# The sample group's window state in a one-step decoder kernel: copied from DRAM to DRAM during the first MLP instead of stored from attention's buffers

## The chip, the cores and the metric

The kernel runs on one core of a Trainium2 chip, as one launch. The metric is device time in microseconds (us), the median of several executions. In what follows PE is the tensor engine, DVE the vector engine, ACT the scalar engine, POOL the GpSimd engine and SP the sync engine. SP does no arithmetic: it issues DMA transfers in the order in which they stand in its program, and where one of them has to wait for a semaphore, all that stand behind it wait too. ACT and POOL can issue transfers as well.

## What is computed

One step of a two-layer trunk runs for two groups with the same weights. The prompt group is one sequence of 512 new tokens; the sample group is eight sequences (DEC_BATCH = 8) with one new token each and 2048 cached ones. The first layer mixes by pooling, then comes an MLP; keys and values are computed once; the second layer is attention over three branches (compressed rows, selected pages, a sliding window of 512) with 16 heads, then comes an MLP and the last norm.

```
h -> pool mixer -> sq_relu_mlp            (first layer)
k, v rows <- kv_side(h)
h -> attention(compressed, selected pages, window) -> sq_relu_mlp -> rmsnorm
outputs: y of both groups, the prompt group's new rows and buffers,
         the sample group's new rows, its pool buffer
         and its updated window buffer, win_kv_sample (8, 512, 2, 4, 64)
```

The last of these is what the change is about. In the kernel its key part and its value part are the DRAM tensors `o["wink"]` and `o["winv"]`, and the old window is `a_in["wink"]` and `a_in["winv"]`: each has 8 sequences of 512 KB, 4 MB in all. What is kept of the old window goes on unchanged to the updated buffer, 16 pieces of 512 KB in all.

## The kernel before

All numbers are float32. A product of weights with activations is made from two parts of each (`whi` and `wlo`, written by ACT and DVE), so one product of 1024 by 128 weights is 24 pairs of matmuls on PE.

**Phase A** (0 to about 597 us) holds the pooling layer, the first MLP and the compressed rows of the sample group's cache. `mlp_jobs` makes the MLP's list of jobs: four quarters of eight up products and eight down products. `Job.after` is code that is emitted right behind a job's work on PE. Weights come by SP into a ring of three buffers `wraw` of 512 KB (line 204), are split by ACT (line 215, `whi`) and by DVE (line 195, `wlo`), and the compressed rows' pages (`craw`, line 421) come on SP between them.

**Phase B** (to about 727 us) makes keys, values and queries. **Phase C** (727 to 961 us) is attention. **Phase D** is the output projection, the second MLP and the last norm.

In phase C one list scheduler orders everything (`attend` lists the steps, `emit` orders them). Each step has an engine, an estimated cost and a due time; on each engine that step is emitted which is due first among those that can start by the estimates. The two groups' work is mixed on PE in this way. For the prompt group PE computes scores (`sc`, line 1069), transposes of the weights (`pt`, line 1215) and products with the values (`pv`, line 1252), 28 `pv` matmuls per head. For the sample group PE reads 40 halves, which we number here:

- K0 to K3 are the scores against the window's keys, K4 to K19 those against the selected pages (line 1446, 16 `sv` matmuls each);
- V0 and V1 are the products with one half of the window's values, V2 to V17 those with the selected pages, V18 and V19 those with the other half of the window (line 1541).

Each half needs two buffers of 512 KB. They come from a ring of six, three `wraw` (the weights' buffers) and three `kvs`, filled by SP: a window's buffer by one transfer (line 1412), a pages' buffer by three or four transfers of one page (line 1417, a page's number read from a table first) while POOL fetches the page that is left (line 1421). So two buffers of pages are seven loads on SP.

For the window's halves there is a step more, `kept`: behind the PE step it puts on SP the two stores (`keep`, line 1433) of the same buffers into `o["wink"]` or `o["winv"]`, and then a step that stands for their transfer. Both touch the buffers, so to the scheduler a buffer is free only when the store is over. At the end of the phase SP loads the output projection's first weights into the three `wraw` buffers (line 204), and DVE's split of them (`wlo`) stands in DVE's order ahead of the sample group's last steps (`sx`, `sos`).

Of the kernel before, what the change touches and what calls it, by code (L numbers as in the profile page):

```python
# [17 lines left out]
NT = T + DB  # L18
# [7 lines left out]
# The list scheduler's aims in the attention phase, in microseconds: the end of head n is due at PERIOD * (n + 1) + LATE,  # L26
# the sample group's products evenly from FIRST on; BIAS shifts a head's kinds of steps against each other (scores,
# maxima, weights, sums, transposes, their high and low parts). ORDER: the chunks of the sample group's values.
# [4 lines left out]
# The order of the pooling layer: K a job of the sample group, s a step on the vector engine behind it, n the norm, u a  # L33
# product. FILLERS: the sample group's jobs behind each product of the first MLP.
# [3 lines left out]
# The order of the key and value products and the queries' with what stands between them; how many jobs later than the  # L38
# next each of their finishing steps comes; those whose rotation is the vector engine's.
# [8 lines left out]
class Buf:  # L48
    """One turn of a buffer: its kind, and the ops that touch it, the one that takes it among them."""
# [5 lines left out]
class Op:  # L55
    """A step on one engine: what emits it, about how long it takes, which ops it follows, which buffers it touches;
    due: when it has to be over, as far as its followers don't tell; lag: what its followers wait behind its end."""
# [9 lines left out]
def emit(ops, rings, taken=()):  # L67
    """Emits the ops as a list scheduler orders them: on each engine the one that is due first of those that can
    start. rings: buffers per kind; taken: buffers in use from the start."""
# [14 lines left out]
    def start(o):  # L84
        """The earliest start as far as it is known."""
        t = now
        for p in o.after:
            if p.end is None:
                return None
            t = max(t, p.end + p.lag)  # L90
        want = {}
        for b in o.bufs:
            old = turns[b.kind]
            if b in old:
                continue
            x = len(old) + want.get(b.kind, 0) - rings[b.kind]
            want[b.kind] = want.get(b.kind, 0) + 1
            if x >= 0:
                for u in old[x].users:
                    if u.end is None:  # L100
                        return None
                    t = max(t, u.end + 0.1)
        return t
# [29 lines left out]
class Job:  # L133
    """One stretch of work on the tensor engine, with what comes before it and after it. loads: (kind, function)
    pairs, one buffer each; frees: {kind: n}, the buffers that prep or pe is the last to read; post may be several
    functions, each a job later than the one before it; after comes right behind pe; no prep comes ahead of a job
    with bar."""
# [8 lines left out]
def trunk(tc, a, o):  # L146
# [17 lines left out]
    # ---- what lives through the whole program  # L164
# [32 lines left out]
    # ---- weights: raw from DRAM, then the two parts that float32r carries exactly  # L197
# [27 lines left out]
    def gemm(ps, w, xs, koff=0, m=128, cols=(0, 1)):  # L225
        """ps [m, 2, 512] = w' x over the k tiles; xs gives (hi, lo) [128, NT] of each."""
        n = len(xs)
        for k, (xh, xl) in enumerate(xs):
            for wt, x in ((w.hi, xh), (w.hi, xl), (w.lo, xh)):
                for i in cols:  # L230
                    TE.matmul(ps[0:m, i, 0:NH], wt[:, koff + k, 0:m], x[:, i * NH:(i + 1) * NH],  # L231
                              start=(k == 0 and wt is w.hi and x is xh), stop=(k == n - 1 and wt is w.lo))
# [5 lines left out]
    def run(js, ahead=1, done=0):  # L238
        """done: so many preps are out already."""
# [15 lines left out]
        def preps(i):  # L255
            """What is due once job i is on the tensor engine: the next ahead preps, none from behind a bar."""
# [44 lines left out]
    # ---- RMS norms  # L301
# [5 lines left out]
    def sq_acc(ct, rows=None):  # L307
        """Adds the squares of h's tile ct to the sums."""
        if ct == 0:
            S.activation(accn, h[:, 0], AF.Square)  # L310
            return
        q = tmp()
        S.activation(q, h[:, ct], AF.Square)
        V.tensor_add(accn, accn, q)
# [22 lines left out]
    def scaled(gi, ct):  # L337
        """The two parts of h's tile ct times the norm's weights; the products' columns take the rest of the norm."""
# [6 lines left out]
    # ================= phase A: pooling layer, first MLP, the sample group's compressed rows  # L345
# [49 lines left out]
    def pages(k, n):  # L395
        """The n page numbers from position k of the table."""
# [15 lines left out]
    def cmp_job(b, e, rq):  # L412
        """Two of the eight row pairs of one sequence's segments; the last one finishes the hidden rows."""
# [41 lines left out]
        # the values' rows: x0, x1 the even and the odd segments, A, B the two parts of the weights; a window of two  # L455
        # segments is A x0 + B x1 = (A - B) (x0 - x1) + A x1 + B x0 or A x1 + B x0 of the next pair
# [100 lines left out]
    def take(n):  # L557
        """The next n pieces of the sample group's work (a finishing step goes with the piece before it)."""
# [10 lines left out]
    # ---- pooling layer  # L569
# [6 lines left out]
    def first_norm():  # L576
        """h's sums of squares, added up on the tensor engine."""
# [110 lines left out]
    # ---- an MLP: four quarters of the hidden features, each summed into the residual  # L688
    def mlp_jobs(l, filler, done, before=lambda: None):
# [28 lines left out]
        for q in range(4):  # L718
            for f in range(8):
                js.append(gemm_job(W(a["up"][l, 8 * q + f]), xpairs, up_post(8 * q + f), kind=kind))  # L720
                if q == f == 0:
# [15 lines left out]
    def last_quarter(xs):  # L737
        """The last products and the final norm, one half of the rows after the other, so that the first half's norm and
        stores run beside the second half's products; the weights stay on chip for both."""
# [61 lines left out]
    # ================= phase B: K/V side and the queries  # L801
# [175 lines left out]
    # ---- queries: one head's two parts stacked on the partitions  # L977
# [82 lines left out]
    # ================= phase C: attention  # L1060
    hd_of = lambda t, s: ((2 * s + t // 4) * 4 + t % 4)

    def s_jobs(t, s):
        """Scores and weights of one head, for the query tiles 0 and 1, 2, 3: window and selected keys side by side, the
        compressed rows in front; those of tile 3 go with tile 2's."""
# [106 lines left out]
    def early(k):  # L1172
        """A score job of head 0, among the queries' products."""
# [22 lines left out]
    # the blocks of 128 keys by 128 queries that are transposed together: (branch, key tile, query tile), branch 0 the  # L1196
    # compressed rows; their products with the values: (branch, key tile, the two blocks), block -1 one of zeros
# [9 lines left out]
    def t_steps(t, s, p, kind):  # L1207
        """Transposes of the weights of two query tiles, into the two parts of a tile of values' weights."""
# [65 lines left out]
    # ---- the sample group's attention  # L1274
# [25 lines left out]
    def own():  # L1300
        """The sample group's bank."""
# [5 lines left out]
    def qk16(ps, n, rhs):  # L1307
        """ps [128 rows, n] = the rows' queries times rhs(b, gl), four sequences side by side on the array."""
# [87 lines left out]
    def stream():  # L1396
        """A buffer for two sequences' 256 keys; the weights' buffers serve here too."""
# [5 lines left out]
    def fetch(box, z, q, c, cache, window):  # L1403
        """Pages 2c and 2c + 1 (or 256 of the window's rows) of sequences z + 4q and z + 4q + 2."""
# [20 lines left out]
    def two(window, z, q, c):  # L1425
        """256 rows of two sequences in a window's buffer."""
        w = window.rearrange("b c p n -> c p b n") if len(window.shape) == 4 else window.rearrange("b c p i n -> c p b (i n)")
        return w[c - 8, :, z + 4 * q:z + 4 * q + 3:2]

    def keep(box, z, c, stored):  # L1430
        """The window's rows go on to the updated buffer."""
        for q in range(2):
            nc.sync.dma_start(two(stored, z, q, c), box["t", z, q].rearrange("p x i n -> p x (i n)"))
# [4 lines left out]
    def sk_steps(c, box):  # L1438
        """Scores against 256 cached keys; c < 8 the selected branch's pages, 8 and 9 the window's."""
# [38 lines left out]
    # the softmax over the selected (1) or the window's (2) keys, in pieces; the last column is the new token's  # L1478
# [114 lines left out]
    # ---- the order of all that: one list of steps, put on the engines by when they are due  # L1593
    def attend(wos):
# [19 lines left out]
        # the prompt group  # L1614
# [40 lines left out]
        # the sample group: its steps on the tensor engine are due evenly  # L1655
# [6 lines left out]
        def moved(n, mb, lag):  # L1662
            """The transfer behind a step that starts it."""
# [14 lines left out]

        def kept(box, z, c, to, after, bufs):
            op("SP", 1.0, lambda: keep(box, z, c, to), [after], bufs)  # L1680
            moved(bufs, 1.05, 1.6)
# [23 lines left out]
        def keys(c):  # L1705
# [3 lines left out]
            for z in range(2):  # L1709
                ls, bufs = loads(c, z, a_in["selk"], a_in["wink"], box)  # L1710
                a = pe_op(1, 1.1, lambda z=z: pe(z), ls + [a], bufs + [tok])
                if c >= 8:
                    kept(box, z, c, o["wink"], a, bufs)
# [23 lines left out]
        for c in ORDER:  # L1737
# [4 lines left out]
            for z in range(2):  # L1742
                ls, bufs = loads(c, z, a_in["selv"], a_in["winv"], box)
                halfs.append(pe_op(1, 0.97, lambda z=z, half=half: half(z), ls + [a, first], bufs + [x, sv]))
                if c >= 8:
                    kept(box, z, c, o["winv"], halfs[-1], bufs)
# [15 lines left out]
        # the output projection's first weights  # L1762
# [14 lines left out]
    # ================= phase D: output projection, second MLP, final norm  # L1777
# [148 lines left out]
```

## Time and profile before

| | us |
|---|---|
| median of 3 runs | 1389.64 (1389.13 to 1391.23) |
| profiled execution, first to last instruction (span) | 1390.0 |
| phase A, first MLP within it | 0 to about 597 |
| attention (phase C) | about 727 to 961 |
| first and last half of the sample group read by PE | K0 752.1, V19 ends 951.3 |

The only time of the profiled execution is its span; it lies within the three runs. Times in the trace count from the span's start. A row with a count such as x16 is that many instructions in a row. "A <- B: 5.0, 3, 4.4" means that A stood waiting for B for 5.0 us in total, three times, at most 4.4 us at once.

### The profile page before, as it was taken

To read this page: it belongs to the slowest core of one execution; us is meant where nothing else is said; L and a number is where in the kernel's file an instruction comes from. 1 tells how busy PE (TensorE), PEld (TensorE's weight loads), DVE (VectorE), ACT (ScalarE), POOL (GpSimd) and SP (SyncE) were. 2 spreads that over 40 slices of the span, in tenths; PEclk is the share of its full clock that TensorE was granted. 3 is DMA by queue.
4 is the path that set the end of the run, shared out by engine and by line. 5 is a ranking of instruction groups with operands and counts; after the bars stand their busy time and mean duration, and the time that the engine had idled before them with its cause. 6 is when DMAs were issued, how large, how long until landed. Compare 5 with 4: busy or idle time off the path is not lost.

```text
span 1390.0 us, 27785 instructions
## 1 busy us (share of the span) xinstructions
PE 1344.3 (97%) x10843; PEld 1263.7 (91%) x10843; DVE 845.3 (61%) x1338; ACT 585.3 (42%) x1120; POOL 183.7 (13%) x264
## 2 busy tenths in 40 slices
PE   7999999999999999999997999998999999999997
PEld 6788999999999999989985777777999999999996
DVE  2788766565565476556789977764554353453563
ACT  4555443333233243464445867773432222221231
POOL 0000000000000000012354755660000000000000
PEclk9999999999999999999998999999999999999999
DMA  8755244434424232349506678778323333333231
GB/s 262 223 153 185 78 135 137 122 91 138 136 68 147 76 107 77 92 138 231 141 16 239 204 209 266 213 209 279 91 89 93 93 93 97 92 93 92 92 91 62
DMA packets 114397, 189.56 MB, mean 136 GB/s; under 512 B 13641, under 2 KB 81482, under 8 KB 113882
## 3 DMA queue, kind: packets, MB, share of 16 engines
q1 hardware_dynamic: 106554, 175.04, 41.1%
q0 software_dynamic: 7168, 12.21, 3.5%
q8 instruction: 86, 1.41, 0.4%
q10 hardware_dynamic: 544, 0.53, 0.1%
q14 instruction: 45, 0.37, 0.1%
HBM read 169.20 MB, written 16.43 MB: 134 GB/s over the span
## 4 chain that ended last, share of the span: by engine, by line
PE 88%; DVE 4%; ACT 2%; SPq 2%; DMA 2%; issue 1%; POOL 0%; DVEq 0%; ACTq 0%; POOLq 0%
PE mm L231 65%; PE hid L445 6%; PE hid L488 5%; PE pv L1252 3%; PE sc L1069 3%; PE pt L1215 2%; PE sv L1541 1%; PE sv L1446 1%; SPq L1417 1%; DVE sm L1088 1%; PE hid L915 1%; PE aux L523 1%; PE aux L584 1%; DVE QOb L195 0%; ACT P L1096 0%
## 5 line engine op out<-in xcount | busy, mean ns | idle before, releaser
L231 PE MATMUL mm<-xn,whi 128*128 128x260 f32 (+1 forms) x2784 | 450.2, 284 | 0.4 <-DVE xn L195 0.3
L231 PEld LDWEIGHTS mm<-xn,whi 128*128 128x128 f32 (+1 forms) x2784 | 383.5, 189 | 1.7 <-DVE xn L195 0.5
L195 DVE TENSOR_TENSOR wlo<-wraw,whi 128x1024 fp32r<-128x1024 f32 x163 | 200.7, 1231 | 259.1 <-ACT whi L215 258.8
L231 PE MATMUL mm<-at,whi 128*128 128x260 f32 x2048 | 332.7, 281 | 0.3 <-DVE at L195 0.3
L215 ACT ACTIVATE whi<-wraw 128x1024 fp32r<-128x1024 f32 x163 | 171.6, 1052 | 315.4 <-PE mm L231 259.5
L231 PEld LDWEIGHTS mm<-at,whi 128*128 128x128 f32 x2048 | 283.9, 188 | 1.0 <-DVE at L195 0.5
L231 PE MATMUL mm<-xn,wlo 128*128 128x260 f32 (+1 forms) x1392 | 281.1, 283 | 0.0
L231 PE MATMUL mm<-at,wlo 128*128 128x260 f32 x1024 | 216.0, 282 | 0.0
L231 PEld LDWEIGHTS mm<-xn,wlo 128*128 128x128 f32 (+1 forms) x1392 | 215.2, 188 | 0.0
L231 PEld LDWEIGHTS mm<-at,wlo 128*128 128x128 f32 x1024 | 161.4, 188 | 0.0
L195 DVE TENSOR_TENSOR clo<-craw,chi 128x512 fp32r<-128x512 f32 x128 | 85.4, 687 | 43.3 <-ACT chi L433 28.2
L704 ACT ACTIVATE at<-tmp 128x520 fp32r<-128x520 f32 x64 | 40.9, 639 | 144.1 <-DVE tmp L702 144.1
L1096 ACT ACTIVATE P<-sc,sm 128x512 f32<-128x512 f32 (+2 forms) x192 | 83.4, 453 | 13.5 <-DVE sm L1088 9.8
L1109 POOL TENSOR_TENSOR P<-P,sm 128x1024 f32<-128x1024 f32 (+1 forms) x64 | 80.2, 1263 | 24.1 <-DVE sm L1102 16.9
L705 DVE TENSOR_TENSOR tmp<-tmp 128x520 f32<-128x520 f32 x64 | 44.8, 701 | 45.1 <-ACT at L704 45.1
L1215 PEld LDWEIGHTS pt<-cst,P 128*128 128x128 f32 x384 | 44.0, 144 | 25.3 <-issue 8.7
L1215 PE MATMUL pt<-cst,P 128*128 128x128 f32 x384 | 58.0, 284 | 9.2 <-POOL P L1109 4.9
L810 POOL MEMSET V2c<- 128x512 f32 x1 | 0.5, 525 | 482.2 <-DMA wraw<-in_wkv_dram 482.2
L781 POOL TENSOR_TENSOR h<-h,rn 128x260 f32<-128x260 f32 x2 | 1.9, 944 | 443.2 <-ACT rn L776 443.2
L702 DVE SCALAR_TENSOR_TENSOR tmp<-mm,rn 128x520 f32<-128x520 f32 x64 | 44.5, 695 | 26.1 <-PE mm L231 21.6
L1088 DVE TENSOR_REDUCE sm<-sc 128x2 f32<-128x1024 f32 (+2 forms) x96 | 54.8, 615 | 6.4 <-PE sc L1069 5.9
L433 ACT ACTIVATE chi<-craw 128x512 fp32r<-128x512 f32 x64 | 37.0, 624 | 49.9 <-PE hid L445 33.2
(283 smaller groups left out, 1972.6 us busy)
## 6 DMA issues: line engine op xcount, KB each, us to landing
craw<-in_cc_dram SPq DMA_DIRECT2D x256, 128.0 KB, 2.5
wraw<-in_up_dram SPq DMA_DIRECT2D x64, 512.0 KB, 3.6
wraw<-in_down_dram SPq DMA_DIRECT2D x64, 512.0 KB, 3.6
wraw<-in_selk_dram SPq DMA_DIRECT2D x59, 128.0 KB, 2.2
wraw<-in_selv_dram SPq DMA_DIRECT2D x59, 128.0 KB, 2.8
kvs<-in_selk_dram SPq DMA_DIRECT2D x53, 128.0 KB, 3.1
kvs<-in_selv_dram SPq DMA_DIRECT2D x53, 128.0 KB, 2.3
wraw<-in_wkv_dram SPq DMA_DIRECT2D x12, 512.0 KB, 3.5
```

Source lines behind the costliest of these rows:

```text
L195: V.tensor_tensor(out, x, hi.bitcast(F32), op=OP.subtract)
L215: S.activation(hi, raw, AF.Copy)
L231: TE.matmul(ps[0:m, i, 0:NH], wt[:, koff + k, 0:m], x[:, i * NH:(i + 1) * NH], start=(k == 0 and wt is w.hi and x is xh), stop=(k == n - 1 ...
L445: TE.matmul(box["ps"][:, 0:508], wt[:, wk], x[:, r, 4 * p:4 * p + 508], start=(rq == 0 and r == 0 and p == 0 and wt is w1hi and x is part[ ...
L488: TE.matmul(out, wt, x, start=(k == 0 and m == 0 and n != 1), stop=(k == 7 and m == 2), skip_group_check=True)
L702: V.scalar_tensor_tensor(halves(r), view(ps), 0.0, halves(rn), op0=OP.max, op1=OP.mult)
L705: V.tensor_mul(r, r, r)
L1069: TE.matmul(out, l, r, start=start, stop=stop, skip_group_check=True)
L1088: V.tensor_reduce(sm[:, c:c + len(outs)], src, axis=AX.XY if len(src.shape) == 4 else AX.X, op=OP.max, negate=True)
L1096: S.activation(dst, x, AF.Exp, bias=sm[:, c:c + 1], accum_out=sm[:, m + c:m + c + 1])
L1109: G.tensor_tensor(x, x, sm[:, c:c + 2, None].to_broadcast(list(x.shape)), op=OP.mult)
L1215: TE.transpose(ps[:, 128 * x:128 * x + 128], ab["P", t, s, q][:, c:c + 128], ident)
```

## The change

`keep` and `kept` go, and with them the 16 stores on SP. In the first MLP, behind each of the eight up products of the second quarter ACT issues one copy of a sequence's old window keys straight from DRAM to DRAM, and in the third quarter one of its values: 16 copies of 512 KB. The diff also blanks comments and docstrings, which is left out here; line numbers of the changed kernel differ by 2 or 3.

```
-    def keep(box, z, c, stored):
-        """The window's rows go on to the updated buffer."""
-        for q in range(2):
-            nc.sync.dma_start(two(stored, z, q, c), box["t", z, q].rearrange("p x i n -> p x (i n)"))
-
...
-        def kept(box, z, c, to, after, bufs):
-            op("SP", 1.0, lambda: keep(box, z, c, to), [after], bufs)
-            moved(bufs, 1.05, 1.6)
...
                 a = pe_op(1, 1.1, lambda z=z: pe(z), ls + [a], bufs + [tok])
-                if c >= 8:
-                    kept(box, z, c, o["wink"], a, bufs)
...
                 halfs.append(pe_op(1, 0.97, lambda z=z, half=half: half(z), ls + [a, first], bufs + [x, sv]))
-                if c >= 8:
-                    kept(box, z, c, o["winv"], halfs[-1], bufs)
...
         for q in range(4):
             for f in range(8):
                 js.append(gemm_job(W(a["up"][l, 8 * q + f]), xpairs, up_post(8 * q + f), kind=kind))
+                if not l and q in (1, 2):
+                    js[-1].after = lambda x=("wink", "winv")[q - 1], b=f: S.dma_start(o[x][b], a_in[x][b])
```

On ACT, in the second quarter of the first MLP, the changed kernel's program reads as follows; nothing of it but the copies is new, and the other engines' programs are unchanged up to attention:

```order
115 L215 ACTIVATE whi<-wraw 128x1024 x2
116 L722 DMA out_wink_dram<-in_wink_dram 16x8192
117 L467 ACTIVATE chi<-craw 128x8x4x16 x2
118 L471 ACTIVATE dhi<-tmp 128x512
119 L704 ACTIVATE at<-tmp 128x520
120 L722 DMA out_wink_dram<-in_wink_dram 16x8192
121 L215 ACTIVATE whi<-wraw 128x1024
```

The copies stand among ACT's weight splits. Some of them, and some of SP's loads behind them, wait for an earlier transfer, since transfers share eight completion semaphores.

On SP, at the start of attention, the kernel before has:

```order
590 L1412 DMA wraw<-in_wink_dram 128x2x512 x3
591 L1412 DMA kvs<-in_wink_dram 128x2x512 x3
592 L1433 DMA out_wink_dram<-wraw 128x2x512 x3
593 L1433 DMA out_wink_dram<-kvs 128x2x512 x3
594 L1412 DMA wraw<-in_wink_dram 128x2x512 x2
595 L397 TENSOR_LOAD ptab
```

and the changed kernel has in this place:

```order
590 L1414 DMA wraw<-in_wink_dram 128x2x512 x3
591 L1414 DMA kvs<-in_wink_dram 128x2x512 x3
592 L1414 DMA wraw<-in_wink_dram 128x2x512 x2
593 L397 TENSOR_LOAD ptab
594 L1419 ISA
```

The stores between the loads are gone, here and in the three other places where stores stood; the order of SP's loads is the same in both. Which turn of the ring a buffer takes has changed: the first page buffer of K6 takes in the kernel before the place of one of K4's buffers, and in the changed kernel that of one of K3's.

On PE, early in attention (the prompt group's head 1 is being finished), the kernel before has:

```order
2575 L1252 MATMUL pv<-whi,V_6881 128x256 x8
2576 L1069 MATMUL sc<-Kd,h 128x512 x3
2577 L1069 LDWEIGHTS identb
2578 L1069 MATMUL sc<-masks,identb 128x256
2579 L1069 MATMUL sc<-Kd,h 128x512
2580 L1215 MATMUL pt<-cst,P_8762 128x128
```

and the changed kernel:

```order
2575 L1254 MATMUL pv<-whi,V_6897 128x256 x8
2576 L1443 MATMUL sv<-wraw,Qpad 32x256 x8
2577 L1217 MATMUL pt<-cst,P_8778 128x128
2578 L1217 MATMUL pt<-cst,P_8777 128x128
2579 L1217 MATMUL pt<-cst,P_8778 128x128 x2
2580 L1071 MATMUL sc<-Kd,h 128x512 x3
```

Half K3 (row 2576, `sv`) now stands straight behind this head's first `pv`; before it stands at row 2610, behind 16 more `pt`, 20 more `pv` and 13 more `sc`. From here to the middle of the values the sample group's halves stand further ahead among the prompt group's work. Counted from the start of attention, so many of the prompt group's matmuls stand ahead of a half:

| half | before: pt, pv, sc | changed: pt, pv, sc |
|---|---|---|
| K3 | 56, 56, 91 | 40, 36, 78 |
| K4 | 68, 64, 104 | 64, 56, 99 |
| K19 | 200, 224, 217 | 164, 176, 204 |
| V0 | 208, 232, 230 | 192, 214, 230 |
| V10 | 288, 326, 314 | 296, 326, 314 |
| V12 | 316, 364, 330 | 316, 364, 330 |

From V12 on the two orders are the same on PE, and so are those of DVE, ACT and POOL from about there. SP's loads of the output projection's first weights follow the last window loads directly in the changed kernel; before, the four last stores stand between them, and the second and third of those weight loads wait for such stores.

## Rows read from the trace of the kernel before

**Rows 1.** The page's busy time of each engine over the whole span, and the chain of work that ended last, as shares of the span by engine (SPq is SP's queue).

```profile
PE 1344.3 (97%) x10843; PEld 1263.7 (91%) x10843; DVE 845.3 (61%) x1338; ACT 585.3 (42%) x1120; POOL 183.7 (13%) x264
...
PE 88%; DVE 4%; ACT 2%; SPq 2%; DMA 2%; issue 1%; POOL 0%; DVEq 0%; ACTq 0%; POOLq 0%
```

**Rows 2.** Windows: the length of a stretch, then busy time (and instructions) of PE, PE's weight loads, DVE, ACT and POOL in it, the granted clock, the DMA engines' mean busy share and GB/s. The first stretch lies in the first MLP, the others in attention.

```profile
300.00:360.00 60.00, 60.00 (x503) 59.48 (x502) 33.98 (x53) 19.61 (x28) 0.00 (x0) 1.00 0.37 110
...
760.00:800.00 40.00, 39.82 (x348) 31.89 (x337) 37.19 (x82) 30.84 (x105) 25.63 (x32) 0.96 0.72 226
800.00:840.00 40.00, 37.70 (x326) 27.59 (x325) 26.89 (x60) 25.16 (x80) 23.31 (x29) 1.00 0.70 207
840.00:880.00 40.00, 38.74 (x359) 29.13 (x357) 33.51 (x74) 31.59 (x110) 22.23 (x29) 1.00 0.83 262
```

**Rows 3.** What SP's queue waited for between 240 and 420 us, in the first MLP: the weight loads wait for DVE to be done with a buffer.

```profile
SPq L204 <- DVE wlo L195: 132.0, 20, 11.4
```

**Rows 4.** DMA issues grouped by line: count, KB each, median us from issue to landing. A weight load of the first MLP, a page load of the keys, and a store of the kind that goes.

```profile
wraw<-in_up_dram SPq DMA_DIRECT2D x64, 512.0 KB, 3.6
...
kvs<-in_selk_dram SPq DMA_DIRECT2D x53, 128.0 KB, 3.1
...
out_wink_dram<-wraw SPq DMA_DIRECT2D x5, 512.0 KB, 7.8
```

**Rows 5.** SP's timeline, 740 to 850 us: start, length and count of each run of issues of one kind.

```profile
748.60 2.96 SPq L1433 DMA_DIRECT2D out_wink_dram<-wraw  x3
752.54 3.02 SPq L1433 DMA_DIRECT2D out_wink_dram<-kvs  x3
...
767.54 4.87 SPq L1417 DMA_DIRECT2D kvs<-in_selk_dram  x7
777.37 6.58 SPq L1417 DMA_DIRECT2D wraw<-in_selk_dram  x11
...
847.05 1.37 SPq L1417 DMA_DIRECT2D kvs<-in_selk_dram  x3
```

**Rows 6.** The same from 850 to 962 us, where the values are loaded.

```profile
858.70 2.17 SPq L1433 DMA_DIRECT2D out_winv_dram<-kvs  x2
...
864.08 4.33 SPq L1417 DMA_DIRECT2D kvs<-in_selv_dram  x7
...
937.89 1.37 SPq L1417 DMA_DIRECT2D kvs<-in_selv_dram  x3
...
951.35 10.28 SPq L204 DMA_DIRECT2D wraw<-in_wo_dram  x5
```

**Rows 7.** All that SP's queue waited for between 777.4 and 848.4 us (the wait of 4.4 us is the one that ends at 777.37).

```profile
SPq L1417 <- PE sv L1446: 5.0, 3, 4.4
SPq L1417 <- PE pv L1252: 0.3, 2, 0.2
```

**Rows 8.** What SP's queue waited for between 864 and 939.3 us, the two largest of five rows.

```profile
SPq L1417 <- PE pt L1531: 1.4, 3, 0.7
SPq L1417 <- PE pt L1215: 1.1, 4, 0.3
```

**Rows 9.** What PE waited for, from 760 to 861 us (first row) and from 861 to 961 us.

```profile
PE sv L1446 <- DMA kvs<-in_selk_dram: 2.0, 2, 1.0
...
PE pt L1570 <- DVE sos L1566: 3.1, 1, 3.1
...
PE sv L1541 <- DMA kvs<-in_winv_dram: 1.2, 1, 1.2
PE sv L1541 <- DMA kvs<-in_selv_dram: 0.7, 1, 0.7
```

**Rows 10.** The chain of waits in order of time, pieces with start and length: K4 and the prompt group's work behind it, then the end of attention.

```profile
776.34 1.00 PE sv L1446 x16
777.34 0.59 PE pt L1215 x4
777.93 1.17 PE pv L1252 x10
779.10 0.44 PE pt L1215 x4
779.54 1.12 PE sc L1069 x8
...
784.98 1.07 PE sc L1069 x5
...
951.35 4.61 DMA wraw<-in_wo_dram
...
957.13 1.23 DVE wlo L195
```

**Rows 11.** PE's timeline: the matmuls of K2, then the prompt group's head behind it; K19 begins; V0; and the products with the new tokens' values at the end (the idle time before a row stands in brackets).

```profile
759.63 1.04 PE L1446 MATMUL sv<-kvs,Qpad 128*32 128x256 f32 x12
...
763.84 0.87 PE L1069 MATMUL sc<-Kd,h 128*128 128x512 f32 x3
...
851.37 0.41 PE L1446 MATMUL sv<-wraw,Qpad 128*32 128x256 f32 x2
...
858.59 1.07 PE L1541 MATMUL sv<-kvs,spt 128*32 128x256 f32 x16 [0.31 <-ACT spt L1535]
...
955.19 1.99 PE L1559 MATMUL sv<-VN,PNT 8*128 8x256 f32 x8
```

## The prediction

> **What bounds the kernel now.** The page comes first. PE is busy for 97% of the span and carries 88% of the chain that ended last [rows 1], so time is gained or lost only where PE stands idle or where the order of its work changes. Next the windows by stage: in the first MLP PE is busy without a gap while ACT works a third of the time and the DMA engines are 37% busy; in attention PE loses 2.3 of 40 us and 1.3 of 40 us in two stretches that hold the loads of keys and values [rows 2]. The waits say what for: 2.0 us for pages of the keys, 1.9 us for values and window values, and 3.1 us at the very end, behind DVE [rows 9].
>
> Then SP's timeline. From 777.37 us to the end of the last key load at 848.42 us SP issues loads without rest [rows 5]; within these 71.0 us only 0.9 us is waiting for a free buffer (the 4.4 us end before it) [rows 7]. These are the halves K6 to K19, 28 buffers: 70.1 / 28 = 2.50 us a buffer, 5.0 a half. The values' stretch, 864.08 to 939.26 us, holds 15 halves, 30 buffers [rows 6], with waits of 2.5 us in its two largest rows [rows 8]: 72.7 / 30 = 2.42 us. So keys reach PE at the pace of SP's issuing, and the DMA engines behind are 70% busy [rows 2]. The attention stage has two limits close together: PE's mixed work, and SP's page loads.
>
> **The 16 copies in the first MLP: 0.** Each is one issue on ACT. The nearest rows are SP's stores of the same size, three in 2.96 us, 1.0 us each [rows 5]; ACT has 40 us free in 60 [rows 2]. Behind a copy on ACT stand the weights' splits, and PE and DVE wait for those. Some copies wait for an earlier load (3.6 us from issue to landing [rows 4]), and some of SP's later loads for a copy. The cover is the weights' lead: SP itself stands 132 of 180 us waiting for a weight buffer to come free, up to 11.4 us at once [rows 3], so a load that is some 4 us late still comes ahead of its use. The 8 MB that they move (4 MB of keys, 4 MB of values) meet DMA engines that are 37% busy. A gain is excluded, since PE has no gap there to fill; the upper bound is about five delays of 1 us where ACT's wait falls just ahead of a split that PE needs: +5. I take 0.
>
> **The stores on SP: earlier pages.** Eight issues before 768 us go, 3.0 + 3.0 us and two more, with the waits for landing in front of them [rows 5]. At once K6's first buffers take the place of K3's and not of K4's, so they wait for K3's read. In the new order K3 stands where the first scores behind K2 stand now, at 764.0 us, and is read by 765.0 [rows 11]. K4 comes behind 24 pt, 20 pv and 21 sc. At 0.11 us per pt (0.15 more behind an sv), 0.117 per pv, 1.07 per five sc and 1.12 per eight [rows 10] that is 2.8 + 2.3 + 3.3 = 8.4 us: read from 773.4 to 774.4, where it was 776.3 to 777.3. By then SP has done two buffers of K6; 26 are left for K19. They wait for buffers that K4 to K16 free.
>
> **PE's order: the sample group further ahead.** Between K4 and K19 PE had 132 pt, 160 pv, 113 sc, and now has 100, 120 and 105: by the same prices 3.5 + 4.7 + 1.1 = 9.3 us less. What took from 777.3 to about 852.4 (75.1 us, the 2.0 us of waiting in it) now takes about 75.1 - 2.0 - 9.3 = 63.8 us at most, to 838.2. But SP needs 26 x 2.50 = 65.0 us behind 774.4 and the last page 3.1 us to land [rows 4]: 842.5. K19 is read to 843.5, and PE stands idle some 5 us in place of 2. The lead that the scheduler gives is more than SP can follow; its estimate of SP's issuing (1.7 and 2.3 us a buffer, 2.0 in the mean, in the code of `loads`) is below the 2.50 that the rows show.
>
> Between K19 and V0 the new order has 28 pt, 38 pv, 26 sc, where 8, 8 and 13 stood: 3.1 + 4.4 + 4.4, and as before the products with the compressed values (16 sv, 1.0) and three transposes (0.3): 13.2 us, and 0.3 for the split that V0 waited for [rows 11]. V0 comes at 857.0 to 857.4, where it was 858.6: **-1.2** with the upper value.
>
> Behind V0 the new order still has what it put off: 16 pt and 18 pv more, 1.8 + 2.1: **+3.9**. All of it lies ahead of V12, on PE, and nothing hides it but PE's waits in this stretch.
>
> **The values' side: -1.9.** Four stores at 858.70 to 862.3 us and the wait to 864.08 go [rows 6], so SP starts the page loads some 4 us earlier against a PE that reaches V12 later; the waits for values (0.7) and window values (1.2) [rows 9] should end. Bound: 0 if the loads again wait for buffers, as much as 1.9 if not. I take all.
>
> **The end: -1.2.** The first load of the output projection lands 4.6 us behind the last sv, and DVE's split of it ends at 957.13 + 1.23 = 958.36 us [rows 10]; the sample group's last step stands behind that split, while its products are done at 955.19 + 1.99 = 957.18 us [rows 11]. Without the four stores this load waits for an earlier read and meets no stores' traffic; then the products are next, 1.2 us earlier. More is not to be had there.
>
> **The sum**, against the profiled span of 1390.0 (0.4 above the median): -1.2 + 3.9 - 1.9 - 1.2 = -0.4 us. On the median: 1389.2 us. With 2.42 us a buffer K19 and V0 are 2.1 us earlier: -2.5. Without any relief on the values' side and at the end: +2.7. The forecast's own range is 1387.1 to 1392.3. A measurement of this kernel tells about 0.2%, 2.8 us, from no change, so this forecast is "the same".
>
> **Rivals.** (1) *Faster: SP's issuing is no limit.* If a free ring lets the loads run closer than 2.50 us a buffer, PE never waits in the keys' stretch. PE's work is the same, so what can be saved is what it waits for transfers: 2.0 + 0.7 + 1.2 [rows 9] and 1.2 at the end: -5.1, 1384.5. It needs 63.8 - 3.1 = 60.7 us for 26 buffers, 2.33 each; the rows' 2.42 and 2.50 speak against it, the 8.4 us between K3 and K4 and the missing traffic of 8 MB of stores for it. The Trainium skill, page "DMA: Bandwidth & Descriptors", section "Issuing engines are not separate DMA queues", has a rule that leads here: the sequencer's time to initiate a transfer is usually small relative to the transfer itself. The trace disagrees for these page loads: 2.50 us of issuing for three or four of 128 KB that land in 2 to 3 us together.
>
> (2) *Slower: the lead is not kept.* The 5 us idle are paid, the prompt group's put-off work comes late, and V's loads, which need buffers that PE frees, come late with it, so that both waits of the values stay. The point is V0 at 860 us or later, 2.6 us a buffer: +1.4 + 3.9 - 1.2 = +4.1, 1393.7. For it: a wait in an in-order queue is rarely made up, and DVE, 37.2 of 40 us busy at 760 to 800 [rows 2], is not moved at all and could hold K4 back. Against it: SP has less to do in every stretch.
>
> (3) *Slower: the copies disturb the first MLP*, by the waits on ACT and SP named above: +5, 1394.6. PE without a gap [rows 2] speaks for it, the weights' lead [rows 3] against.
>
> **How the numbers follow.** Forecast 0.48, of which 0.02 each falls beyond 2.8 us on either side; faster 0.24; slower by the lead 0.18; slower by the copies 0.10. Faster by over 0.2%: 0.24 + 0.02 = 0.26; within: 0.44; slower: 0.18 + 0.10 + 0.02 = 0.30. The range runs from the faster rival's price, 1384.5, to the copies', 1394.6; what lies beyond either is about 2 in 10.
>
> **What the profile after would show.** The first MLP: PE busy 60.00 of 60 us as before and phase A as long. SP: key loads back to back from about 765 us, with a break before K4, ending near 840 at 2.5 us a buffer. PE: idle in front of the keys' sv some 5 us, K19 near 843, V0 near 857, no wait for values, and less than 3.1 us in front of the last transposes. Wrong would be the forecast if V0 came before 854 or after 860 us, if PE had gaps in the first MLP, or if the end behind V19 were as long as before.

## The result

| | us | ratio to the kernel before, 95% interval |
|---|---|---|
| before, 4 runs beside it | 1390.43 median (1389.13 to 1392.97) | |
| changed, 4 runs | 1399.41 median (1398.34 to 1400.98) | 1.0060 [1.0044, 1.0075] |

The change costs 0.6%, 8 to 9 us. This lies outside the forecast's own range (1387.1 to 1392.3) and above the slowest rival's price (1394.6). The profiled execution's span is 1399.1 us against 1390.0.

First the page of the changed kernel: busy time by engine, and the shares of the chain that ended last (compare [rows 1]).

```profile
PE 1348.8 (96%) x10843; PEld 1264.4 (90%) x10843; DVE 843.6 (60%) x1338; ACT 585.8 (42%) x1120; POOL 184.6 (13%) x264
...
PE 87%; DVE 4%; ACT 3%; SPq 2%; DMA 2%; issue 1%; POOL 0%; DVEq 0%; ACTq 0%; POOLq 0%
```

The same instructions, and PE's share has fallen by a point. Where it fell is seen in the windows (compare [rows 2]; columns as there).

```profile
300.00:360.00 60.00, 60.00 (x503) 59.48 (x503) 33.97 (x53) 19.42 (x28) 0.00 (x0) 1.00 0.42 126
360.00:420.00 60.00, 60.00 (x502) 59.48 (x501) 38.53 (x59) 22.62 (x32) 0.00 (x0) 1.00 0.57 176
...
760.00:800.00 40.00, 38.32 (x335) 29.27 (x336) 33.17 (x76) 27.32 (x94) 26.44 (x33) 0.97 0.60 175
800.00:840.00 40.00, 37.90 (x310) 26.02 (x310) 26.66 (x58) 24.17 (x82) 21.88 (x29) 1.00 0.70 207
840.00:880.00 40.00, 38.58 (x340) 29.23 (x335) 29.19 (x68) 30.68 (x104) 22.35 (x29) 1.00 0.56 175
880.00:920.00 40.00, 35.64 (x317) 27.06 (x315) 26.71 (x58) 27.57 (x95) 22.59 (x31) 1.00 0.66 192
```

Two rows of the kernel before that [rows 2] does not have:

```profile
360.00:420.00 60.00, 60.00 (x501) 59.48 (x501) 38.54 (x59) 22.20 (x32) 0.00 (x0) 1.00 0.39 115
...
880.00:920.00 40.00, 38.73 (x346) 30.01 (x343) 27.77 (x59) 29.86 (x100) 25.27 (x34) 1.00 0.73 218
```

In the first MLP PE is busy for 60.00 of 60 us although the copies raise the DMA engines' share from 39% to 57%: nothing is lost there. Attention is where it goes. Between 880 and 920 us PE is busy for 35.64 us instead of 38.73. Between 800 and 840 us it is busy for 37.90 us, about as before, but gets through 310 matmuls instead of 326. A matmul of a half lasts 0.38 us in the trace (the 379 ns below are the median), and the next one starts long before its end: sixteen of them take 1.07 us together [rows 11]. So a wait for a page in the middle of a half shows as idle time only as far as it outlasts the matmul before it. (The busy time of PE is thus no measure of its work; the count beside it says more.)

The sample group's matmuls by line (keys, then values), of the changed kernel: least, median and longest duration in ns, then the first and the last start:

```profile
L1443 PE MATMUL sv<-kvs,Qpad x152: 376/379/634, 752.9 to 845.1; 128*32 128x256 f32 x152
...
L1538 PE MATMUL sv<-kvs,spt x160: 379/379/404, 861.0 to 960.3; 128*32 128x256 f32 x160
```

K19 ends some 7 us earlier than before (851.37 us was its first start [rows 11]), but V0 comes at 861.0 instead of 858.59 [rows 11], and the last of V19 starts at 960.3 where the load of the output projection that follows it stood at 951.35 [rows 6]. So V0 is 2.4 us late and the end of the values 9.

PE's waits in attention, 727 to 972 us (compare [rows 9]); the first row is the kernel before's, which [rows 9] does not have:

```profile
PE sc L1069 <- ACT P L1096: 1.3, 1, 1.3
...
PE sc L1071 <- ACT P L1098: 6.2, 6, 1.5
...
PE sc L1071 <- DVE wlo L195: 1.4, 1, 1.4
PE sv L1443 <- DMA kvs<-in_selk_dram: 1.3, 3, 0.8
PE sv L1443 <- DMA wraw<-in_selk_dram: 0.7, 1, 0.7
...
PE sv L1538 <- DMA wraw<-in_winv_dram: 0.2, 1, 0.2
```

The waits for values have nearly gone (1.9 to 0.2 us). A wait that the prediction did not have is now the largest: the prompt group's scores (`sc`) wait 6.2 us for ACT's exponentials (`P`), in six places; before it was 1.3 us in one. They wait 1.4 us more for a split on DVE.

Since the rows show only a part of a wait inside a half, the halves' own lengths tell more. Worked out from the starts in the traces, the 36 halves K4 to K19 and V0 to V19 together take 9.4 us beyond 1.07 us each in the kernel before (keys 5.3, values 4.1) and 11.8 in the changed one (keys 9.6, values 2.2).

SP's timeline of the changed kernel, the places that answer to [rows 5] and [rows 6]:

```profile
764.85 13.05 SPq L1419 DMA_DIRECT2D wraw<-in_selk_dram  x11
...
841.12 1.37 SPq L1419 DMA_DIRECT2D kvs<-in_selk_dram  x3
...
848.10 19.76 SPq L1419 DMA_DIRECT2D kvs<-in_selv_dram  x10
...
947.24 1.37 SPq L1419 DMA_DIRECT2D kvs<-in_selv_dram  x3
...
959.44 11.02 SPq L204 DMA_DIRECT2D wraw<-in_wo_dram  x5
```

SP starts K6's pages at 764.85 instead of 777.37 us and finishes the keys at 842.49 instead of 848.42: of the 12.5 us that it gained at the start, 5.9 are left, since it waits 4.6 us for K4's read within the first row, to 774.88 us, and the issuing itself goes no faster: 67.6 us for the 26 buffers behind it, 2.60 each. At the values it waits for V0 (the row of 19.76 us), and its last page is issued 9 us later than before.

Two pieces of the chain of waits, in order of time: K19, and one of the six places in front of the scores.

```profile
841.65 2.20 DMA kvs<-in_selk_dram
...
843.99 1.50 PE sv L1443 x12
...
895.11 0.69 DVE whi L195
...
895.83 0.69 DVE ot L1267
...
896.56 1.24 DVE sm L1090
...
897.88 0.12 ACT P L1098
...
898.46 0.87 ACT P L1098 x3
...
899.37 1.40 PE sc L1071 x8
```

K19 is read as its pages land: twelve of its matmuls take 1.50 us where sixteen took 1.00 [rows 10]. And the scores at 899.37 us start when the exponentials of the scores before them, which hold a score buffer, are over. ACT's timeline of this place says how these come late (idle time in brackets):

```profile
893.30 0.60 ACT L1228 ACTIVATE wlo<-pt 128x512 fp32r<-128x512 f32 x1 [2.65 <-PE sv L1538]
894.48 0.60 ACT L1228 ACTIVATE whi<-pt 128x512 fp32r<-128x512 f32 x1 [0.58 <-PE pv L1254]
...
896.56 0.64 ACT L1270 ACTIVATE QOb<-ot 128x512 fp32r<-128x512 f32 x1 [0.87 <-DVE ot L1267]
...
897.88 0.69 ACT L1098 ACTIVATE P<-sc,sm 128x512 f32<-128x512 f32 x1 [0.20 <-DVE sm L1090]
```

ACT stood idle for 2.65 us behind two halves on PE and then did the splits of the head before. The exponentials at 897.88 us waited for the maxima of the scores (`sm`, on DVE from 896.56 us, a step of the chain above), and DVE took these behind its own part of the splits. So PE waits for ACT, ACT for DVE, and both had waited for PE.

### The profile page after: what moved, and what is told of

Same layout as the page of the kernel before. It is cut to its first block, busy times and chain, and to the rows that moved or that the text cites. A ratio compares the mean times of both kernels' runs of the same rounds, so it can differ in the third digit from the quotient of the medians.

```text
span 1399.1 us, 27765 instructions
## 1 busy us (share of the span) xinstructions
PE 1348.8 (96%) x10843; PEld 1264.4 (90%) x10843; DVE 843.6 (60%) x1338; ACT 585.8 (42%) x1120; POOL 184.6 (13%) x264
## 4 chain that ended last, share of the span: by engine, by line
PE 87%; DVE 4%; ACT 3%; SPq 2%; DMA 2%; issue 1%; POOL 0%; DVEq 0%; ACTq 0%; POOLq 0%
PE mm L231 64%; PE hid L445 6%; PE hid L488 5%; PE sc L1071 2%; PE pt L1217 2%; PE pv L1254 2%; PE sv L1538 1%; SPq L1419 1%; PE sv L1443 1%; DVE sm L1090 1%; ACT P L1098 1%; PE aux L523 1%; PE hid L917 1%; DMA wraw<-in_winv_dram 1%; PE aux L584 1%
```

## The experiments

**The theory** after these rows: the new order of the work in attention costs the time, because the sample group's keys run further ahead than SP's page loads can follow and what is put off is then done with less between its dependent steps. **Rivals:** the copies (ACT's issues, shared semaphores, traffic), and the missing stores themselves. The runs went in three groups, each beside the kernel before on the same chip, so they are compared by their ratio to it; 0.0010 is 1.4 us. All stand on the changed kernel, apart from e4.

**e1, e2, e3, e4: order, copies and stores apart.** The scheduler is given the steps of `kept` again, which emit nothing. Then PE, DVE and POOL have exactly the program of the kernel before, ACT has it with the copies, and SP has that of the changed kernel.

```
+        def kept(box, z, c, to, after, bufs):
+            op("SP", 1.0, lambda: None, [after], bufs)
+            moved(bufs, 1.05, 1.6)
...
+                if c >= 8:
+                    kept(box, z, c, o["wink"], a, bufs)
...
+                if c >= 8:
+                    kept(box, z, c, o["winv"], halfs[-1], bufs)
```

> The stores are gone and the 16 copies stand in the first MLP, as in the changed kernel, but the scheduler still gets the steps of kept, which now emit nothing: every engine's order in attention is that of the kernel before. Theory (the new order of PE's work costs the time, neither the copies nor the missing stores do): 1386 to 1390 us, that is before (1390.4) less 0 to 4 us for SP's free queue and the earlier output projection weights. Rival (the copies disturb the first MLP, or transfers go later into attention): 1397 to 1401 us, as the changed kernel. If both had a share it would lie near 1394.

e2 leaves the copies out of the changed kernel, e3 out of e1:

```
-                if not l and q in (1, 2):
-                    js[-1].after = lambda x=("wink", "winv")[q - 1], b=f: S.dma_start(o[x][b], a_in[x][b])
```

> The changed kernel without the 16 copies; the updated window buffer is not written at all. Order as in the changed kernel. Theory (order): 1398 to 1400 us, as with the copies. Rival (copies): 1388 to 1391 us.

> Neither stores nor copies, and the order of the kernel before, by steps of kept that emit nothing; the updated window buffer is not written. Theory (order): the same as with the copies, within 1 us, 1386 to 1390 us; against the kernel before this is what the 16 stores themselves cost on SP and the DMA engines. Rival (copies): 2 us or more below the run with the copies and the old order.

e4 is the kernel before with these two lines added.

> The kernel before, with its stores, and the 16 copies in the first MLP as well, so the window buffer is written twice with the same values. Order as in the kernel before. Theory (order): 1390.4 us, no change within 1 us. Rival (copies): 1397 to 1400 us.

| | order | stores | copies | us, median | ratio, 95% interval |
|---|---|---|---|---|---|
| changed | new | no | yes | 1399.41 | 1.0060 [1.0044, 1.0075] |
| e2 | new | no | no | 1400.73 | 1.0061 [1.0047, 1.0075] |
| e1 | old | no | yes | 1386.61 | 0.9961 [0.9946, 0.9976] |
| e3 | old | no | no | 1386.28 | 0.9959 [0.9944, 0.9973] |
| e4 | old | yes | yes | 1390.73 | 0.9990 [0.9978, 1.0002] |

The copies cost nothing in either order. Taking the stores away is worth 0.39%, 5.4 us, if the order stays. The order alone costs 1.0060 - 0.9961 = 0.0099, 13.8 us. e1 does all that the change means to do and is faster than both kernels. What its PE waits for in attention, of the kinds above:

```profile
PE sc L1071 <- ACT P L1098: 1.3, 1, 1.3
...
PE sv L1443 <- DMA kvs<-in_selk_dram: 1.2, 2, 0.9
...
PE sv L1538 <- DMA kvs<-in_winv_dram: 0.5, 1, 0.5
```

Its keys and values:

```profile
L1443 PE MATMUL sv<-kvs,Qpad x152: 376/379/603, 753.4 to 849.7; 128*32 128x256 f32 x152
...
L1538 PE MATMUL sv<-kvs,spt x160: 379/379/403, 856.2 to 946.5; 128*32 128x256 f32 x160
```

K19 is read 4.6 us later than in the changed kernel, and the values end 13.8 us earlier.

**e5, e6: which part of the order.** The empty steps for the keys alone (e5: the keys' order of before, from V1 on an order of its own), or for the values alone (e6: the keys as far ahead as in the changed kernel).

Against e1:

```
(e5)
-                if c >= 8:
-                    kept(box, z, c, o["winv"], halfs[-1], bufs)
(e6)
-                if c >= 8:
-                    kept(box, z, c, o["wink"], a, bufs)
```

> The changed kernel, but the scheduler gets the empty steps of kept for the window's keys alone. The order is that of the kernel before up to V1 (K19 behind 200 pt, 224 pv); from there on it differs from both (V4 behind 232 pt, 260 pv; V8 as before). Theory (the lead that the sample group's keys get over SP's page loads is what costs: PE waits for pages up to K19, and behind it the prompt group's scores, now without the halves between them, wait for ACT's exponentials): the lead is gone, so 1386 to 1389 us. Rival (any order that the scheduler makes without the constants being fitted to it loses): 1391 us or more.

> The changed kernel, but the scheduler gets the empty steps of kept for the window's values alone. The keys stand as far ahead as in the changed kernel (K19 behind 164 pt, 176 pv); the values stand nearer to the kernel before (V4 behind 232 pt, 260 pv, V8 behind 272 and 308). Theory (the lead of the keys is what costs): 1395 to 1400 us. Rival (the order of the values, behind V4, costs): 1390 us or less.

e5: 1385.21 us, 0.9953 [0.9938, 0.9968], the fastest of those that do the whole work. e6: 1395.29 us, 1.0034 [1.0021, 1.0048]. The order of the values alone costs nothing when the keys stay (0.9953 against 0.9961), and e5's order of the values is not one that the constants were fitted to: such an order need not lose. The lead of the keys costs 1.0034 - 0.9961 = 0.0073, 10.2 us; with it, the values' order of the changed kernel adds 0.0026, 3.6 us. The scores' wait in e6 stands between those of e1 (1.3 us) and of the changed kernel (6.2 us, and 1.4 for DVE, which e6 does not have):

```profile
PE sc L1071 <- ACT P L1098: 3.9, 4, 1.3
```

**e9: the scheduler's estimate of SP.**

```
-                x = op("SP", 0.5 if c >= 8 else 1.7 if rest else 2.3, load, [opened], [buf])
+                x = op("SP", 0.5 if c >= 8 else 2.2 if rest else 2.8, load, [opened], [buf])
```

> The changed kernel with the scheduler's estimate of SP's page loads raised from 1.7 and 2.3 us a buffer to 2.2 and 2.8, about the 2.5 in the mean that SP took. K19 then stands behind 200 pt and 224 pv, as in the kernel before, K8 behind 84 and 84. Theory (the lead over SP costs): 1386 to 1391 us. Rival (an order for which the constants weren't fitted): 1394 us or more.

1389.80 us, 0.9989 [0.9979, 0.9998]: 1.0060 - 0.9989 = 0.0071, 9.9 us of the order's 13.8, are gone by raising the estimate alone, though K3 and K4 stay where the changed kernel has them and nothing else was fitted. It is 0.0028, 3.9 us, behind e1.

**e7, e8, e10: pages that cost SP little.** One transfer per buffer of pages that lie next to each other, in place of three or four transfers and the table's reads (other pages, as many bytes); in e10 for all four pages, with nothing left for POOL. e7 and e10 have the order of the changed kernel, e8 that of e1.

```
-            pgs = pages(DB * NPAGE + k, by_sp) if c < 8 else ()
+            if c < 8:
+                nc.sync.dma_start(t.rearrange("p x i n -> p (x i) n")[:, 0:by_sp], cache[k:k + by_sp].rearrange("o p n -> p o n"))
...
-                for i in range(2) if c < 8 else ():
-                    if 2 * x + i < by_sp:
-                        nc.sync.dma_start(t[:, x, i], cache[ds(pgs[2 * x + i], 1)].rearrange("o p n -> (o p) n"))
(e10: the load takes all four pages, and POOL none)
+                nc.sync.dma_start(t.rearrange("p x i n -> p (x i) n"), cache[k:k + 4].rearrange("o p n -> p o n"))
...
-            for n in range(by_sp, 4):
+            for n in range(0):
```

> The changed kernel in its own order, but SP loads the three or four pages of a buffer by one transfer from pages that lie next to each other, without reading the table: the pages are the wrong ones, the bytes the same. SP then needs some 1 us a half in place of 5. Theory: the waiting for pages up to K19 goes (4 to 7 us), the prompt group's waits behind it stay: 1391 to 1395 us. Rival 1 (SP's issuing is no limit, the order alone costs): 1398 to 1400 us. Rival 2 (all of the loss is SP's issuing): 1386 us or less.

> The same single transfer per buffer (wrong pages, same bytes) in the order of the kernel before, by the empty steps of kept, with the copies. Theory: there PE waits little for pages, so 1384 to 1386.5 us against 1386.6 with the page loads; the changed order with one load stays 6 to 10 us above this one. Rival 1: no difference between one load and four in either order, and 13 us between the orders. Rival 2: the two orders within 2 us of each other.

> The changed kernel in its own order, with all four pages of a buffer by one transfer on SP (wrong pages, same bytes) and nothing left for POOL to fetch. Against the run with one load of SP's own pages (1392.6) PE's wait for POOL's pages, 2.0 us by its profile, should go: 1389 to 1391.5 us. What is then left above the old order with cheap loads (1382.2) is the order of the work alone, with no wait for a page: theory 6 to 9 us, in front of the prompt group's scores. Rival (the pages' arrival is all): 1384 us or less.

| | order | pages | us, median | ratio, 95% interval |
|---|---|---|---|---|
| e7 | new | one load on SP | 1392.63 | 1.0012 [1.0001, 1.0023] |
| e10 | new | all by that load | 1389.12 | 0.9981 [0.9971, 0.9992] |
| e8 | old | one load on SP | 1382.17 | 0.9933 [0.9917, 0.9948] |

In the new order the pages' way is worth 1.0060 - 0.9981 = 0.0079, 11.0 us (6.7 by SP's issues, 4.3 by POOL's pages, which come next once SP's are early); in the old one 0.9961 - 0.9933 = 0.0028, 3.9 us. So 11.0 - 3.9 = 7.1 us of the order's 13.8 are pages that come too late for the lead. With no page late the new order is still 0.9981 - 0.9933 = 0.0048, 6.7 us slower. e7's first waits in attention, then e10's, then e8's:

```profile
PE sc L1071 <- ACT P L1098: 6.4, 6, 1.5
...
PE sv L1441 <- DMA kvs<-in_selk_dram,idx: 2.0, 2, 1.1
```

```profile
PE sc L1071 <- ACT P L1098: 6.8, 7, 1.5
...
PE sc L1071 <- DVE wlo L195: 1.4, 1, 1.4
```

```profile
PE sc L1071 <- ACT P L1098: 1.3, 1, 1.3
```

In e10 no wait for a page is left. The scores wait 6.8 us for ACT and 1.4 for DVE against 1.3 in the old order, where the wait for DVE does not occur: 6.9 us more, which accounts for the 6.7. e8, lower than expected (1384 to 1386.5), still has POOL's pages, but none of its waits names them.

The lengths of the halves, reckoned as above, say the same of the pages: beyond 1.07 us each they take 11.8 us in the changed kernel, 4.8 in e7 and nothing in e10; in the old order 4.8 in e1 and 0.7 in e8. The order thus costs 11.8 - 4.8 = 7.0 us in late pages, beside the 7.1 from the runs' times. In e9 the halves lose nothing either, so the 3.9 us by which it lies behind e1 are not late pages.

**e12, e13: is it the maxima?** In both all four pages come by one load, as in e10; e12 has the new order, e13 the old one.

```
-                    V.tensor_reduce(sm[:, c:c + len(outs)], src, axis=...
+                    V.tensor_reduce(sm[:, c:c + len(outs)], src[..., 0:src.shape[-1] // (2 if t >= 4 else 1)], axis=...
```

> As the run before, and for the later eight heads DVE takes the maxima over the first half of each block of scores alone, which shortens the step between the scores and ACT's exponentials (the results of attention differ). Theory (behind the lead PE waits for scores' banks, which come free only after DVE's maxima and ACT's exponentials): 2 to 5 us less than the run before. Rival (other waits, or none, set the pace there): within 1 us of it.

> The same shorter maxima and the same page loads in the order of the kernel before (empty steps of kept). Theory: there the scores hardly wait, so it is within 1.5 us of the old order with one load a buffer (1382.2). Rival (shorter maxima help any order): 2 us or more below it.

e12: 1385.83 us, 0.9963 [0.9949, 0.9977], 2.5 us below e10. e13: 1379.49 us, 0.9914 [0.9899, 0.9929], 2.6 us below e8 (which differs from it in POOL's pages as well; PE did not wait for those). The theory had e12 right (2 to 5 us), but e13 was to gain less than 1.5 us. Both orders gain about the same, as far as intervals of some 2 us either way tell, so the length of the maxima does not explain the difference between the orders. The wait for exponentials in e12 is no shorter than in e10 (the 1.4 us for DVE have gone):

```profile
PE sc L1071 <- ACT P L1098: 7.4, 8, 1.3
```

What makes the exponentials late was then read from the traces of the changed kernel and of e1 alone: what ACT waits for from V0 to V12 in each (861 to 931 us, and 856 to 917), first the changed kernel.

```profile
ACT whi L1228 <- PE pv L1254: 6.1, 5, 2.2
ACT wlo L1228 <- PE pt L1217: 5.2, 3, 2.6
ACT wlo L1228 <- PE sv L1538: 2.7, 1, 2.7
ACT whi L1228 <- PE pt L1217: 2.1, 3, 1.0
```

```profile
ACT whi L1228 <- PE pt L1217: 4.4, 3, 2.1
ACT whi L1228 <- PE pv L1254: 2.2, 3, 1.4
ACT wlo L1228 <- PE pt L1217: 2.1, 3, 0.9
```

In the new order ACT waits 16.1 us for PE in front of its splits of transposed weights (6.1 + 5.2 + 2.7 + 2.1), in the old one 8.7 (4.4 + 2.2 + 2.1); the exponentials, or DVE's maxima ahead of them, queue behind these splits, and PE's scores wait for the exponentials. That PE loses the last 6.7 us in front of its scores is in the rows of e10 and e8. That the splits are why is not shown: no run tried it, and ACT's longer waits for PE can as well be what follows from PE's.

## Why the prediction was wrong

**The copies: 0.** Right: e1 against e3, e4 against the kernel before, and PE at 60.00 of 60 us. The lead of the weights was the right cover to name.

**K4 and the page loads' pace.** Right in kind: K4 was foretold for 773.4 us, and in the changed kernel's trace its first matmul starts at 773.78. The pace behind it was 2.60 us a buffer in place of 2.50, so the keys, which were to be read to 843.5 us, are read to 845.5. PE was to be idle some 5 us in place of 2; by name it waits as long as before, but by the halves' lengths the keys lose 9.6 us in place of 5.3. SP's pace, not PE, set K19, and e7 shows it: the rival "SP's issuing is no limit" falls. The Trainium skill, page "DMA: Bandwidth & Descriptors", section "Issuing engines are not separate DMA queues", has it that the sequencer's time to initiate a DMA is usually small relative to the DMA itself. For this stream of 128 KB loads the runs disagree: three or four issues, with the table's reads, made one are worth 6.7 us here.

**V0: -1.2 foretold, +2.4 measured.** This step failed first. K19 was 2 us later than worked out, and what lies between K19 and V0 took 15.5 us, where the sum of the matmuls' own durations gave 13.5. PE has 1.1 us of waits by name there, 0.7 of it in front of the prompt group's scores; the rest no row names.

```profile
856.57 0.90 PE L1071 MATMUL sc<-Kd,QOb 128*128 128x288 f32 x5 [0.68 <-ACT P L1098]
```

**V0 to the end of V19: 3.9 - 1.9 = +2.0 foretold, +6.6 measured** (99.3 us, 861.0 to 960.3, against 92.7, 858.59 to 951.3). The values' waits did go, 1.7 us of 1.9 by name (4.1 to 2.2 by the halves' lengths). What failed is the +3.9: the put-off work was priced at its matmuls' durations, as if PE had only to get through it. It is a chain across PE, DVE and ACT: in this stretch the scores wait by name 1.1 and 1.5 us for exponentials and 1.4 us for a split on DVE, 4.0 us that the old order does not have. That these waits appear because the sample group's halves were already spent and there was less between the links is argued, not shown. Rival 2 had the right place (V0 at 860 us or later, which the prediction had also named as a sign of being wrong) and a wrong price: it let put-off work cost only its own length, 4.1 us, and kept the values' waits, which in fact went.

**The end: -1.2 foretold, -0.2 measured.** From the last sv to the output projection's first product it took 951.3 to 961.21 us before and takes 960.3 to 970.04 now.

```profile
959.88 4.53 DMA wraw<-in_wo_dram
...
964.89 1.06 ACT whi L215
...
965.98 1.22 DVE wlo L195
```

The first load goes off with the last read, as before, and lands 4.53 us later; the 4.61 us of [rows 10] were not due to the stores' traffic. In e1 the end is as long, 9.8 us.

**The whole.** The three misses, 3.6, 4.6 and 1.0 us, make 9.2 of the 9.5 us between the forecast's -0.4 and the profiled +9.1. The removal of the stores was worth 5.4 us, where the terms for it gave 3.1: in the old order V0 comes 2.4 us earlier (858.59 to 856.2) and the end of the values 4.8 us (951.3 to 946.5), and the halves lose 4.8 us in place of 9.4: the loads are relieved and nothing more is asked of them. The change as made gave that back and 8.4 us more (13.8 - 5.4), by what the scheduler did with the freed engine: its estimates said SP could follow a longer lead. The prediction saw this (2.0 against 2.50 us a buffer) and counted its effect on the page loads, but not on the scores.

**What stays open:** whether the scores' waits are held by the order on ACT and DVE or by the lack of work between the steps. The runs show that they do not come from the pages (e10 against e8), and that the keys' lead alone brings a part of them (1.3 us in e1, 3.9 in e6); the two on ACT behind V0 and the one on DVE are not in e6, so they also need the values' order of the changed kernel.

## What to carry to other kernels

Where a scheduler orders the work, removing a step also removes a constraint, and the new order is a change of its own: run the edit with an empty step in the old place first, which here turned +0.6% into -0.4%. An estimate too low for a busy queue (2.0 us a buffer for 2.5) did its harm when that queue was relieved, and raising it took back 9.9 of 13.8 us; set such an estimate to the duration in the trace before the order is trusted. And put-off work cost more here than its own instructions: price it with the waits of its chain. Last, PE's idle time understates its waits: the starts of a group's matmuls tell more.

## What was not expected of the hardware

Sixteen copies of 512 KB from DRAM to DRAM, beside a stage in which PE never idles, cost nothing measurable (1386.61 us with, 1386.28 without), with the DMA engines at 57% instead of 39% in the stretch that has most of the values' copies. One transfer of three or four 128 KB pages in place of as many transfers, and no table reads, was worth 3.9 us even in the order in which PE waited only 1.2 us by name for such pages: by the halves' lengths it lost 4.8 us there for pages and window values, and 0.7 with the one transfer.
